# A scheduled GLA + RWKV-7 layer: PSUM-bank reads and DMA costs in the scheduler's account, new scheduling numbers, and the edge column copied before the shift

## The chip, the cores and the metric

The kernel runs on one core of one Trainium2 chip. The metric is device time in microseconds (us) of one execution, lower being better. TensorE is called PE here, VectorE is DVE, ScalarE is ACT, GpSimd is POOL, and SP is SyncE, whose instruction queue issues every DMA of this kernel. All data is fp32. Most projections run as three fp32r matmuls per block of weights, high and low parts of weights and inputs being kept apart.

## The reference

One layer of a hybrid decoder: 1024 prompt tokens and 8 sample tokens are projected by one large matrix, go through a gated linear attention branch (4 heads) and an RWKV-7 branch (16 heads), are merged under two sigmoid gates, projected once more and normalised.

```python
p = jnp.einsum('btd,dn->btn', x, w_in)
p_gla, p_rwkv, p_gate = _split(p, (GLA_COLS, RWKV_COLS, GATE_COLS))
...
o_gla, S_gla = _gla_chunked(...)          # chunked causal gated linear attention
...
prev = jnp.concatenate([shift0[:, None, :], p_rwkv[:, :-1]], axis=1)
pr = p_rwkv + (prev - p_rwkv) * rwkv_mu   # token shift: the part that one edit touches
...
y, S_rwkv = _rwkv7_scan(rh, hr(w), kh, vh, kk, hr(a), S_rwkv0)
...
m = (jax.nn.sigmoid(gate_a) * jnp.einsum('btc,cd->btd', o_gla, w_up_gla)
     + jax.nn.sigmoid(gate_b) * jnp.einsum('btc,cd->btd', o_rwkv, w_up_rwkv))
out = jnp.einsum('btd,de->bte', m, w_out)
y_out = _layernorm(DEEPNORM_ALPHA * x + out, ln_g, ln_b, LN_EPS)
```

## The kernel before

**Work and tiling.** Features lie on partitions and tokens on the free axis. The tokens go in two passes: pass 0 has 512 prompt tokens and the 8 sample tokens, cut in tiles of 256 and 264 columns (266 with the lead of the token shift), and pass 1 has the other 512 in one tile. In each pass a list of blocks (`make_plan`, line 1765) names the 128-row blocks of the big projection in order: per pair of RWKV heads (8 pairs) its r, k and v rows, per GLA head its q, k and v rows, the gate rows, and so on. `blocks` (line 726) walks the list: per tile it takes a PSUM bank (`proj`, of which there are 2, or `big`, of which there are 5), and runs 8 input blocks times 3 matmuls into it, the weights being read from four `wpart` buffers of half a block each. Then an evacuating stream reads the bank with ACT and DVE and frees it.

**Weights.** In pass 0 `load_w` (line 667) loads raw weights into `wraw`, ACT copies the high part into `wpart` (a CAST row of the profile), DVE subtracts for the low part, and the result is also stored to DRAM (`w<-wpart`). Pass 1 only reloads it (`wpart<-w`).

**The chain.** `chain` (line 1362) is the serial part of each pair of RWKV heads: 8 chunks, each with three dependent matmuls into the only `pch` bank. After the first, one copy `rh<-pch` by ACT or DVE; after the second, two copies `wide<-pch`, one for each half of the partitions, each by ACT or DVE; after the third, two adds on DVE. `front` (line 1183) prepares a pair: among much else it stores to DRAM (`LD<-gg`), loads back (`wide<-LD`), solves triangles on POOL (`Xt`, `X`) and sends results through DRAM (`XD`, `XT`, `Yd`).

**What sets the order.** No order is written out by hand. Every part of the work is a Python generator that yields one operation at a time, and `Order.run` (line 388) chooses, while the program is being built, which stream's operation is issued next on its engine. It keeps a clock per engine, prices each operation (`price`, line 156; `transfer`, line 217, for DMAs), and works out in `start` (line 351) when it could begin, from when its operands are written and from when its output buffer was last read. The key is that time less a priority (`PRIO`, and `FOR_PE` times a factor for matmuls). Where an operation has two engines to choose from (ACT or DVE, DVE or POOL), the one that would end first gets it, with a handicap (`BIAS` for DVE against ACT, `ASIDE` for POOL). The numbers at the head of the file feed this. Each engine then runs its list strictly in the order of issue, waiting at semaphores.

**The token shift.** `shift` (line 1121) evacuates a projected row of the RWKV branch: ACT writes (1 - mu) times the row, DVE adds mu times the row moved by one token, reading the same PSUM bank, and the last column of the bank is kept in `tail` by ACT, since pass 1 needs the column before its first token. There are 33 such rows in each pass.

**Other names.** `RAWS` (line 61) limits how many raw input blocks `load_x` holds; `EARLY_GATES` (line 70) is compared with an index that runs from 0 to 7 in `load_gates` (line 1577); `GATES` (line 71) says how many gate blocks stand behind each pair, for each pass.

Of the kernel before, what the change touches and what calls it, by code (L numbers as in the profile page):

```python
# [17 lines left out]
PSUM = bass.MemoryType.PSUM  # L18
DRAM = bass.MemoryType.DRAM
# [38 lines left out]
KEEP = 0  # L58
AHEAD = 6

RAWS = 6


WARM = 9
# [2 lines left out]
RANK = 16  # L67
LEAD = 2
SPARE_ROWS = 10
EARLY_GATES = 12  # L70
GATES = [[1, 1, 3, 0, 3, 2, 2, 4], [1, 1, 3, 2, 1, 3, 1, 4]]


HOP = {"P": 0.2, "D": 0.418, "G": 0.115, "V": 0.064, "A": 0.14}

SWITCH = 0.092
HOLD = 0.11
TABLE = 1.28

AGE = 2.117  # L80

SPARE = 0.411
LANDED = 0.648
BIAS = 0.133
ASIDE = 1.655

PRIO = {"evacuate": 0.333, "pair": 0.326, "turn": 0.426, "chain": 0.251, "norm": 0.026, "x": 0.745,
        "lora": 0.67, "rank": 1.291, "head": 0.198, "gate": -0.057, "w": 0.32, "out": 0.555, "state": 0.039,
        "block": 0.735}
FOR_PE = {"pair": 0.438, "turn": 2.001, "chain": 1.193, "norm": 0.187, "lora": 3.947, "rank": 2.131,  # L90
          "head": 0.435, "gate": 1.614, "state": 3.803, "out": 1.518}
STAND, SCARCE, PER_ROW = 0.037, 0.036, 0.042

URGENT = 2.628
SIGMOID, EXP = "sigmoid_and_others", "natural_log_exp_and_others"
SETS = {AF.Sigmoid: SIGMOID, AF.Tanh: SIGMOID, AF.Exp: EXP, AF.Ln: EXP}

# [58 lines left out]
def price(eng, name, out, args, ins):  # L156

    n = out.free_size()
    src = [x for x in ins if x.tensor.space != PSUM] if eng == "A" else ins
    if eng == "P":  # L160
        m = args[0].free_size()
        rows, cols = tiles(name, args)
        if name == "transpose":
            return 0.1095
        if args[0].dtype == F32R:
            return max(m / 1200, 0.0045 + n / 2256) if rows == cols == P else (m + n) / 1200
        if rows == cols == P:
            return 2 * max(m, n) / 1200 + 0.009
        if cols == 32 and n > 2 * P:
            return 0.017 + n / 2326  # L170
        return 0.1365 if cols == P else (0.0625 if cols == 64 else 0.142 if n > P else 0.088) if rows == P else 0.0285 if rows == cols == 64 else 0.5
    if eng == "S":
        return 0.56
    if eng == "A":
        extra = 0.5 * (len(ins) - 1) if src != ins else len(ins) - 1
        return 0.097 + n / 1200 + (0.042 if len(src) == len(ins) else 0.0) + 0.094 * extra
    wide = max([n, *(x.free_size() for x in ins)]) if name in ("tensor_reduce", "bn_stats", "bn_aggr") else n
    if eng == "V":
        if name == "tensor_tensor_scan":
            return 0.1 + n / 480  # L180
        if name == "transpose":
            return 0.17 + n / 960
        if name in ("tensor_copy", "copy", "memset") and ins and ins[0].tensor.space != PSUM:
            wide = wide / 2
        scalars = sum(x.free_size() == 1 for x in ins[1:]) if name in ("scalar_tensor_tensor", "tensor_scalar") else 0
        return 0.068 + wide / (480 if name == "copy_predicated" else 960) + 0.06 * scalars
    if name in ("tensor_scalar", "memset"):
        return 0.08 + n / 760
    return 0.1 + n / (300 if name == "tensor_copy" else 456)
# [27 lines left out]
def transfer(out, src):  # L217

    n = 4 * min(run_of(out), run_of(src), 512 if src.tensor.space == out.tensor.space else 1024)
    return out.nbytes() / n * (0.01 + n * 4.65e-5) / 16, 1.7 if out.tensor.space != DRAM else 1.2  # L220


class Engine:
# [43 lines left out]
class Order:  # L267
# [83 lines left out]
    def start(self, op):  # L351

        best = None
        for eng, fn, cost in op.ways:
            free, t = self.time[eng] + (SWITCH if eng == "P" and op.tiles != self.tiles else 0.0), 0.0
            for x in (*op.outs, *op.ins):
                at, by = self.ready.get(x.tensor.name, (0.0, None))
                if eng == "S" and by == "D" and x is op.out:
                    continue
                if by != eng:  # L360
                    at += HOP.get(by, 0.0) + (SPARE if eng == "P" and by in ("V", "A", "G") else LANDED if by == "D" else 0.0)
                elif eng != "P" and x is not op.out:
                    at += 0.13
                t = max(t, at)
            t = max(t, *(self.read.get(x.tensor.name, 0.0) for x in op.outs))
            if eng in op.port:
                free = max(free, self.port["G" if eng == "V" else "V"])
            late, t = free - t, max(t, free)
            if eng in "VA" and self.held(eng, op):
                cost += HOLD  # L370
            end = t + cost
            if len(op.ways) > 1:
                end += BIAS if eng == "V" and "A" in op.ways[0][0] else ASIDE if eng == "G" and "G" in op.port else 0.0
            if best is None or end < best[0]:
                best = end, t
                op.eng, op.fn, op.cost, op.late = eng, fn, cost, max(0.0, late)
        return best[1]
# [60 lines left out]
class Kern(Order):  # L438
# [682 lines left out]
    def shift(self, c, j, dst, smp=None):  # L1121

        i, A, V = c.i, self.A, self.V
# [3 lines left out]
        def ev(tt, t0, n, q):  # L1127
            np_ = n - c.ns if tt == last else n
            m = n if smp is not None else np_
            lead, e = (LEAD, 0) if tt else (0, 1)  # L1130
            yield lambda: "pv" in self.has
            if i:
                yield lambda: self.edged == NRC
                yield A.activation(dst[:, :1], q[:, :1], AF.Identity, scale=omu, bias=self.tail[:, 0, j:j + 1])
                yield A.activation(dst[:, 1:m], q[:, 1:m], AF.Copy, scale=omu)
            else:
                yield A.activation(dst[:, t0:t0 + m], q[:, lead:lead + m], AF.Copy, scale=omu)
            if i == 0 and tt == last:
                yield A.copy(self.tail[:, :, j], q[:, lead + np_ - 1:lead + n])
            yield V.scalar_tensor_tensor(dst[:, t0 + e:t0 + np_], q[:, lead + e - 1:lead + np_ - 1], mu,  # L1140
                                         dst[:, t0 + e:t0 + np_], ALU.mult, ALU.add)
            if i:
                yield A.copy(self.tail[:, 0, j:j + 1], q[:, n - 1:n])
            elif tt == last:
                self.edged += 1
                if self.edged == NRC:
                    o = PV["mu"][0]
                    yield V.tensor_mul(self.tail[:, 0], self.tail[:, 0], self.pv[:, o:o + NRC])
            if i == 0 and tt == last and smp is not None:
                yield V.scalar_tensor_tensor(smp, self.shT[:, j], mu, dst[:, HT:c.n], ALU.mult, ALU.add)  # L1150
# [754 lines left out]
```

## Time and profile before

| | |
|---|---|
| Median of 3 runs | 1454.28 us (1448.78 to 1454.93) |
| The profiled execution's own time | 1452.62 us |
| Its span, first to last instruction | 1450.8 us |
| DVE busy | 1065.5 us, 2184 instructions |
| ACT busy | 812.0 us, 2019 instructions |
| POOL busy | 385.3 us, 1146 instructions |
| DMA queue, share of 16 engines | 74.2% |

The profiled execution's time lies 1.8 us above its span. PE is almost always busy, so the numbers to read are PE's idle stretches: the view of waits lists them for one engine, by the instruction that ended each wait. A timeline row gives start and duration in us, the engine, the operation, what it writes and reads, and in brackets the idle time before it with what ended that.

### The profile page before, as it was taken

Reading aid. Unit: us, or ns where it says so; the run is one execution under the profiler, and the core shown is the slowest. Engines: PE = TensorE matmul, PEld = TensorE weight load, DVE = VectorE, ACT = ScalarE, POOL = GpSimd, SP = SyncE. Lnnn points to the kernel's source line nnn. Section 1 sums busy time; section 2 is a strip of 40 time slices with the busy share of each in tenths; the row PEclk is TensorE's granted clock in tenths of the full one; section 3 lists DMA queues with packets and bytes.
Section 4 is the critical chain, followed back from the end, with each engine's and each line's share of the span. In section 5 each row is a group of like instructions: output and inputs, shape, how many; then the busy total and the mean of one; then the engine's idle time right before and its main releaser. Section 6 shows DMA issues by size and latency. Waiting matters only on the chain.

```text
span 1450.8 us, 30348 instructions
## 1 busy us (share of the span) xinstructions
PE 1425.3 (98%) x10640; PEld 1251.5 (86%) x10640; DVE 1065.5 (73%) x2184; ACT 812.0 (56%) x2019; POOL 385.3 (27%) x1146
## 2 busy tenths in 40 slices
PE   9999999999999999999999999999999999999997
PEld 8999989999989999878887777887778898898786
DVE  7687578948894778577859786887788655666585
ACT  6565657665757486465564635464556655644210
POOL 1063315150615060505151314324141510000000
PEclk9999999999999999999999999999999999999999
DMA  9788779688877897768576578767786787798732
GB/s 334 254 278 274 234 268 300 225 252 299 284 227 244 279 325 253 205 207 230 176 193 210 147 202 215 235 167 204 212 244 201 227 250 248 238 303 275 260 111 87
DMA packets 284788, 340.12 MB, mean 234 GB/s; under 512 B 159027, under 2 KB 174524, under 8 KB 284636
## 3 DMA queue, kind: packets, MB, share of 16 engines
q1 hardware_dynamic: 284636, 338.18, 74.2%
q8 instruction: 85, 1.39, 0.4%
q14 instruction: 67, 0.55, 0.1%
HBM read 210.03 MB, written 127.00 MB: 232 GB/s over the span
## 4 chain that ended last, share of the span: by engine, by line
PE 83%; DVE 6%; DMA 5%; ACT 3%; SPq 1%; issue 1%; DVEq 0%; ACTq 0%
PE proj L234 52%; PE big L234 26%; PE pch L234 6%; DVE row L234 2%; SPq L234 1%; ACT row L234 1%; DMA wraw<-w_in 1%; DVE wide L234 1%; DMA wpart<-w 1%; DVE gg L234 1%; DMA w<-wpart 1%; DVE wpart L234 1%; DMA gla_s<-row 0%; DMA row<-vd 0%; DMA shift_s<-sto 0%
## 5 line engine op out<-in xcount | busy, mean ns | idle before, releaser
L234 PE MATMUL proj<-xh,wpart 128*128 128x512 f32 (+3 forms) x3680 | 902.2, 329 | 5.7 <-DMA wpart<-w 2.8
L234 PEld LDWEIGHTS proj<-xh,wpart 128*128 128x128 f32 x3680 | 612.8, 188 | 57.7 <-issue 7.6
L234 PE MATMUL proj<-xl,wpart 128*128 128x512 f32 (+3 forms) x1840 | 603.9, 328 | 0.0
L234 PEld LDWEIGHTS proj<-xl,wpart 128*128 128x128 f32 x1840 | 346.7, 188 | 26.0 <-issue 3.3
L234 POOL TENSOR_TENSOR Xt<-X,wide 128x60 f32<-128x60 f32 (+24 forms) x496 | 166.6, 336 | 376.4 <-DMA wide<-LD 191.8
L234 DVE TENSOR_TENSOR wpart<-wraw,wpart 128x512 fp32r<-128x512 f32 x210 | 145.5, 700 | 68.9 <-ACT wpart L234 65.7
L234 ACT CAST wpart<-wraw 128x512 fp32r<-128x512 f32 x210 | 129.2, 620 | 117.4 <-PE proj L234 43.4
L234 DVE TENSOR_TENSOR row<-row 128x512 f32<-128x512 f32 (+8 forms) x339 | 176.4, 532 | 10.8 <-ACT row L234 5.4
L234 POOL TENSOR_TENSOR X<-X,Xt 128x60 f32<-128x60 f32 (+24 forms) x496 | 171.3, 345 | 38.7
L234 ACT ACTIVATE row<-row 128x512 f32<-128x512 f32 (+3 forms) x229 | 137.6, 610 | 14.3 <-DVE row L234 6.8
L234 PE MATMUL big<-xh,wpart 128*128 128x256 f32 (+3 forms) x592 | 136.3, 318 | 0.0
L234 POOL TENSOR_TENSOR row<-row 128x512 f32<-128x512 f32 (+5 forms) x30 | 27.3, 919 | 347.9 <-DVE row L234 195.4
L234 PEld LDWEIGHTS big<-xh,wpart 128*128 128x128 f32 x592 | 98.1, 189 | 7.6 <-issue 0.8
L234 ACT COPY row<-big 128x128 f32<-128x128 f32 (+6 forms) x188 | 61.0, 346 | 61.8 <-PE big L234 52.0
L234 PE MATMUL big<-xl,wpart 128*128 128x256 f32 (+3 forms) x296 | 93.6, 316 | 0.6 <-DVE xl L234 0.6
L234 DVE TENSOR_TENSOR wide<-pch,gg 64x65 f32<-64x65 f32 x224 | 49.6, 222 | 58.3 <-PE pch L234 55.7
L234 ACT COPY rh<-pch 128x130 f32<-128x130 f32 x113 | 30.3, 268 | 107.6 <-PE pch L234 107.2
L234 DVE SCALAR_TENSOR_TENSOR row<-proj,pv,row 128x255 f32<-128x255 f32 (+1 forms) x95 | 54.4, 573 | 34.1 <-ACT row L234 25.4
L234 PE MATMUL big<-row 128*64 128x64 f32 (+5 forms) x680 | 69.7, 287 | 0.5 <-DVE row L234 0.4
L234 ACT COPY wide<-pch 64x65 f32<-64x65 f32 x213 | 44.2, 208 | 44.5 <-PE pch L234 40.5
L234 ACT ACTIVATE row<-proj,omu 128x256 f32<-128x256 f32 (+1 forms) x95 | 51.8, 545 | 25.1 <-PE proj L234 24.5
L416 ACT ACT_TABLE_LOAD x50 | 64.2, 1283 | 0.8
(216 smaller groups left out, 2044.9 us busy)
## 6 DMA issues: line engine op xcount, KB each, us to landing
w<-wpart SPq DMA_DIRECT2D x146, 512.0 KB
wpart<-w SPq DMA_DIRECT2D x146, 512.0 KB
wraw<-w_in SPq DMA_DIRECT2D x146, 256.0 KB
wide<-LD SPq DMA_DIRECT2D x64, 128.0 KB
BT<-row SPq DMA_DIRECT2D x32, 256.0 KB
wide<-BT SPq DMA_DIRECT2D x64, 128.0 KB
wraw<-w_up_gla SPq DMA_DIRECT2D x32, 256.0 KB
row<-w_out SPq DMA_DIRECT2D x32, 256.0 KB
```

Of the source, the lines that this page charges most:

```text
L234: ways.append((eng, lambda call=call: call(out, *args, **kw), price(eng, name, out, args, ins)))
L416: self.nc.scalar.preload_act_table_set(self.table)
```

## The change

The diff has three parts. The first is in the scheduler's account: `start` now also lets an operation that reads PSUM begin only after earlier readers of the same bank; `transfer` makes loads with a broadcast source 2.2 times as long and loads of at most 32 packets of over 2 KB 1.45 times, and stores to DRAM slightly shorter; the issue of a DMA is priced at 0.64 or 0.48 by its number of dimensions in place of 0.56; ACT's fixed cost is lowered from 0.097 to 0.065; a dependent operation on the same engine is spaced by a number for each engine. The second is a new set of scheduling numbers, among them `RAWS`, `GATES` and all priorities. The third is in `shift`: in pass 1 the last column is copied to `tail` ahead of DVE's read of the bank, no longer behind it.

```diff
-RAWS = 6
+RAWS = 5
...
-EARLY_GATES = 12
-GATES = [[1, 1, 3, 0, 3, 2, 2, 4], [1, 1, 3, 2, 1, 3, 1, 4]]
+EARLY_GATES = 16
+GATES = [[3, 1, 3, 1, 2, 3, 2, 1], [2, 1, 3, 5, 0, 1, 4, 0]]
...
+AFTER = {"A": 0.13, "V": 0.13, "G": 0.147, "S": 0.13}
...
-BIAS = 0.133
-ASIDE = 1.655
...
+BIAS = 0.148
+ASIDE = 1.497
...
     if eng == "S":
-        return 0.56
+        return 0.64 if max(sum(int(m) > 1 for _, m in x.ap) for x in (out, args[0])) > 2 else 0.48
     if eng == "A":
...
-        return 0.097 + n / 1200 + (0.042 if len(src) == len(ins) else 0.0) + 0.094 * extra
+        return 0.065 + n / 1200 + (0.042 if len(src) == len(ins) else 0.0) + 0.094 * extra
...
-    return out.nbytes() / n * (0.01 + n * 4.65e-5) / 16, 1.7 if out.tensor.space != DRAM else 1.2
+    packets = out.nbytes() / n
+    slow = 2.2 if any(int(s) == 0 and int(m) > 1 for s, m in src.ap) else 1.45 if packets <= 32 and n > 2048 else 1.0
+    if out.tensor.space == DRAM:
+        return packets * (0.01 + n * 4.2e-5) / 16, 1.2
+    return slow * packets * (0.01 + n * 4.65e-5) / 16, 1.7
...
                 elif eng != "P" and x is not op.out:
-                    at += 0.13
+                    at += AFTER[eng]
                 t = max(t, at)
-            t = max(t, *(self.read.get(x.tensor.name, 0.0) for x in op.outs))
+            t = max(t, *(self.read.get(x.tensor.name, 0.0) for x in (*op.outs, *(y for y in op.ins if y.space == PSUM))))
...
-            if i == 0 and tt == last:
+            if i:
+                yield A.copy(self.tail[:, 0, j:j + 1], q[:, n - 1:n])
+            elif tt == last:
                 yield A.copy(self.tail[:, :, j], q[:, lead + np_ - 1:lead + n])
             yield V.scalar_tensor_tensor(dst[:, t0 + e:t0 + np_], q[:, lead + e - 1:lead + np_ - 1], mu,
                                          dst[:, t0 + e:t0 + np_], ALU.mult, ALU.add)
-            if i:
-                yield A.copy(self.tail[:, 0, j:j + 1], q[:, n - 1:n])
-            elif tt == last:
+            if i == 0 and tt == last:
                 self.edged += 1
```

The program has the same 8925 matmuls before and after. DVE has 47 instructions fewer, ACT 45 more and 10 more table loads (61 in place of 51). Of the 128 copies `rh<-pch`, ACT had 113 and has 125; of the 256 copies `wide<-pch`, ACT had 213 and has 237. Chunks whose two `wide<-pch` copies are split between the engines go from 13 to 7. PE changes its tile size 230 times before and 223 times now.

**First place: ACT in pass 0, at the ninth `rh<-pch` of the chains.** What stands in brackets are the semaphores waited for, DMAHW being those of DMAs. Before:

```order
L234 CAST wpart<-wraw 128x512 [waits DMAHW6_49,DMAHW3_49]
L234 ACTIVATE row<-row 128x256 [waits DMAHW7_49]
L234 COPY rh<-pch 128x130 [waits PE_49]
L234 ACTIVATE gg<-wide,pc 128x130 [waits Activation_49,Pool_49]
L234 COPY row<-proj 128x256 [waits PE_49]
```

And now, from the cast ahead of the same copy on:

```order
L239 CAST wpart<-wraw 128x512 [waits DMAHW6_49,DMAHW7_49,PE_49,Activation_49]
L239 COPY wide<-vm 64x4
L239 ACTIVATE row<-proj 128x128 x2
L239 COPY wide<-vm 64x4
L239 ACTIVATE row<-proj 128x8
L239 COPY wide<-vm 64x4
L239 COPY rh<-pch 128x130 [waits PE_49]
```

The two rows that wait for DMAs stood directly ahead of the chain's copy; now a cast that does so stands six rows ahead of it.

**Second place: ACT in pass 1, at the eleventh edge column.** Before:

```order
L234 ACTIVATE row<-proj,tail,omu 128x1 [waits PE_49]
L234 ACTIVATE row<-proj,omu 128x511
L234 CAST part<-row 128x512 [waits DVE_49]
L234 COPY tail<-proj 128x1 [waits DVE_49]
L234 COPY rh<-pch 128x130 [waits PE_49]
```

And now:

```order
L239 ACTIVATE row<-proj,tail,omu 128x1 [waits PE_49]
L239 ACTIVATE row<-proj,omu 128x511
L239 COPY tail<-proj 128x1 [waits Activation_49]
L239 COPY rh<-pch 128x130 [waits PE_49]
```

The copy of the column waited for DVE's read of the bank with a chain copy behind it; now it follows ACT's own read of the bank.

**Third place: SP in pass 1, where the seventh pair's front stores and reloads `LD`.** Each row issues DMAs; `wpart<-w` are the weights of pass 1. Before:

```order
L234 DMA wpart<-w_1_7557 128x1024
L234 DMA S<-GS_161 128x256
L234 DMA LD_14632<-gg 32x8x32 x4
L234 DMA Ld<-gg 32x4x32 x4
L234 DMA wpart<-w_0_7611 128x1024
L234 DMA wide<-LD_14632 32x1024 x4
```

And now:

```order
L239 DMA wpart<-w_0_7477 128x1024
L239 DMA row<-OS 8x128 x6
L239 DMA wide<-Sp_167 64x65 x2
L239 DMA gla_p<-S 128x256
L239 DMA row<-OS 8x128 x2
L239 DMA row<-sg_105 128x520
L239 DMA wpart<-w_1_7533 128x1024
L239 DMA sg_132<-row 128x512
L239 DMA LD_14715<-gg 32x8x32 x4
L239 DMA Ld<-gg 32x4x32 x4
L239 DMA wide<-LD_14715 32x1024 x4
L239 DMA sg_133<-row 128x512
```

There were 9 other DMAs between two loads of weights and then the four `wide<-LD` behind the second load; now 12 stand ahead of one load, and behind it 15 (the last of them a `BT<-row`, not shown) ahead of the next. Over the whole of SP's list, stretches of 12 or more other DMAs between two loads `wpart<-w` were 6 and are 8.

More of the change, by code (lines that the diff above doesn't have):

```diff
@@ L78 @@
 TABLE = 1.28
-AGE = 2.117
+AGE = 1.487
 SPARE = 0.411
 LANDED = 0.648
-BIAS = 0.133
-ASIDE = 1.655
[L87 to L94, printed above, removed]
+BIAS = 0.148
+ASIDE = 1.497
+PRIO = {"evacuate": 0.383, "pair": 0.309, "turn": 0.598, "chain": 0.413, "norm": 0.266, "x": 0.754,
+        "lora": 0.377, "rank": 1.051, "head": 0.246, "gate": -0.174, "w": 0.3, "out": 0.424, "state": 0.186,
+        "block": 0.718}
+FOR_PE = {"pair": 1.47, "turn": 1.208, "chain": 0.733, "norm": 1.48, "lora": 1.838, "rank": 2.757,
+          "head": 0.983, "gate": 2.698, "state": 2.188, "out": 0}
+STAND, SCARCE, PER_ROW = 0.033, 0.043, 0.107
+URGENT = 1.952
 SIGMOID, EXP = "sigmoid_and_others", "natural_log_exp_and_others"
```

## The prediction

> **What bounds the kernel now.** I read the page first, for the span and the busy shares.
>
> ```profile
> span 1450.8 us, 30348 instructions
> PE 1425.3 (98%) x10640; PEld 1251.5 (86%) x10640; DVE 1065.5 (73%) x2184; ACT 812.0 (56%) x2019; POOL 385.3 (27%) x1146
> PE 83%; DVE 6%; DMA 5%; ACT 3%; SPq 1%; issue 1%; DVEq 0%; ACTq 0%
> ```
>
> PE is busy for 98% of the span, and the chain that ended last is 83% PE. No other engine is near its limit: ACT has 1450.8 - 812.0 = 639 us idle. PE's work doesn't change, so the time moves only by what PE waits. The view of PE's waits lists them; of its 14 rows these are the large ones.
>
> ```profile
> PE pch L234 <- DVE wide L234: 3.0, 5, 1.0
> PE pch L234 <- ACT rh L234: 3.0, 1, 3.0
> PE proj L234 <- DMA wpart<-w: 2.8, 2, 1.4
> PE proj L234 <- DVE row L234: 1.9, 2, 1.7
> PE pch L234 <- DVE rh L234: 1.2, 2, 0.6
> PE big L234 <- DVE Xd L234: 1.1, 1, 1.1
> PE pch L539 <- DVE warm L536: 1.1, 1, 1.1
> PE proj L234 <- ACT row L234: 0.6, 1, 0.6
> PE big L234 <- DVE xl L234: 0.6, 1, 0.6
> PE pch L234 <- ACT wide L234: 0.3, 1, 0.3
> PE big L234 <- ACT l2p L234: 0.2, 1, 0.2
> ```
>
> Each row gives the sum, the count and the longest. These add to 15.8 us, the three other rows to 1.3 more: about 17 us. The wait for `warm` is the start and stays, so some 16 us are all that any order can save by PE's idle time. The rest of PE's idle time is the end:
>
> ```profile
> 1443.04 0.28 PE L234 MATMUL big<-wpart,xl 128*128 128x256 f32 x1
> ```
>
> PE's last matmul ends at 1443.3, and 7.5 us of normalising and storing follow, which the last rows of ACT, DVE and PE in the new order repeat without change. So the question is which of about twenty small waits go, and how many new ones come. A change beyond 0.5% (about what a measurement of this kernel can tell from none) is 7.3 us, nearly half of all that waits.
>
> **Changes of PE's tile size.** They fall from 230 to 223.
>
> ```profile
> 642.09 0.40 PE L234 MATMUL proj<-xl,wpart 128*128 128x512 f32 x1
> 642.32 0.40 PE L234 MATMUL proj<-xh,wpart 128*128 128x512 f32 x1
> 642.65 2.06 PE L234 MATMUL big<-az,wide 64*128 64x128 f32 x32
> ```
>
> From start to start, equal matmuls take 0.23 us and the one ahead of a new tile size 0.33, so a change costs 0.10 us. Seven fewer give **-0.7 us**.
>
> **A cast that waits for a DMA ahead of the chain's copy.** The longest wait is at 188.87.
>
> ```profile
> 187.64 0.62 ACT L234 CAST wpart<-wraw 128x512 fp32r<-128x512 f32 x1 [4.45 <-DMA wraw<-w_in]
> 188.57 0.25 ACT L234 COPY rh<-pch 128x130 f32<-128x130 f32 x1
> 188.87 0.49 PE L234 MATMUL pch<-rh,XT 128*128 128x130 f32 x2 [3.00 <-ACT rh L234]
> ```
>
> ACT stands 4.45 us at the cast for weights that are late; the copy `rh` is queued behind it, and PE has no other work issued ahead of the chain's next matmul. In the first place of the order the cast now stands ahead of that copy with six small instructions between. By the copies here and below, 0.2 us each, that moves the cast about 1.2 us earlier, and as much of the same lateness is off the path. The gain lies between nothing (the weights are later still) and 3.0; I take **-1.2**, the part that the rows show.
>
> **Reads of one bank by two engines.** The scheduler now counts that DVE and ACT read a bank in turn. What that costs when it isn't counted:
>
> ```profile
> 219.55 0.48 DVE L234 SCALAR_TENSOR_TENSOR row<-proj,pv,row 128x256 f32<-128x256 f32 x1 [1.88 <-ACT tail L234]
> 221.15 0.46 PE L234 MATMUL pch<-wide,gg 128*128 128x130 f32 x2 [1.00 <-DVE wide L234]
> 415.30 0.36 PE L234 MATMUL proj<-xh,wpart 128*128 128x266 f32 x1 [1.67 <-DVE row L234]
> ```
>
> At 219.55 DVE stands 1.88 us until ACT has copied the edge column of that bank, the chain's adds come late behind it, and PE waits 1.00. At 415.30 PE waits 1.67 for a bank that DVE still reads. An account that knows of the turn puts other DVE work ahead; but at 219 ACT was itself late by a DMA, and at 415 DVE was behind, which no account of banks mends. Of 2.67 I take half, **-1.3** (ends 0 and -2.7).
>
> **The chain's copies go to ACT.**
>
> ```profile
> L234 ACT COPY rh<-pch x113: 242/268/301, 129.9 to 1241.9; 128x130 f32<-128x130 f32 x113
> L234 DVE COPY rh<-pch x15: 283/294/295, 203.0 to 1156.4; 128x130 f32<-128x130 f32 x15
> L234 ACT COPY wide<-pch x213: 193/208/221, 135.3 to 1243.6; 64x65 f32<-64x65 f32 x107
> L234 DVE COPY wide<-pch x43: 203/219/231, 131.1 to 1230.2; 64x65 f32<-64x65 f32 x43
> 509.74 0.49 PE L234 MATMUL pch<-rh,XT 128*128 128x130 f32 x2 [0.60 <-DVE rh L234]
> ```
>
> The two engines take the same time (268 against 294 ns, 208 against 219), so only the queue counts. Twelve `rh` and 24 `wide` copies leave DVE. The copy whose lateness cost 0.60 at 509.74 is now ACT's: **-0.6**; the other of the two, late in pass 1, stays on DVE. The load that ACT takes on, 36 copies of at most 0.27 us, lies in its 639 us of idle time.
>
> Here a rule of the Trainium skill speaks against the change. The rows first: a split pair.
>
> ```profile
> 879.34 0.21 ACT L234 COPY wide<-pch 64x65 f32<-64x65 f32 x1 [0.87 <-PE pch L234]
> 879.58 0.23 DVE L234 COPY wide<-pch 64x65 f32<-64x65 f32 x1 [2.60 <-ACT wide L234]
> ```
>
> ACT's copy ends at 879.55, DVE's starts at 879.58 and had waited for it; of the 13 split pairs none overlaps. So a split brings nothing, and that the splits fall to 7 costs nothing. The Trainium skill's page "PSUM — Partial Sum Buffer", section "PSUM bank collisions raise a hardware error", says that two engines may use one bank at once in different groups of 32 partitions, and these copies read different halves. By that rule six lost splits would cost six times about 0.2 us, and the sum would come out 1.2 us later; the trace disagrees for this program, and its rows decide.
>
> **Edge column first.** In pass 1 ACT no longer stands at the column for DVE's read.
>
> ```profile
> L234 ACT COPY tail<-proj x64: 150/160/189, 28.4 to 1119.3; 128x1 f32<-128x1 f32 x33, 128x9 f32<-128x9 f32 x31
>   DVE row L234: 25.8, 32
> 1317.02 5.57 PE proj L234 x24
> ```
>
> The second row is the idle time ahead of these copies, 25.8 us in 32 waits, all of it ACT's. DVE's read starts 0.16 us later, 33 times, and the bank comes free a copy earlier. But a tile of pass 1 keeps PE for 5.57 us (last row) with a second `proj` bank besides, and no wait of PE on a bank lies in pass 1. I take **0** (ends: -0.5, the rows `ACT wide` and `ACT l2p`, which are all that PE waits for ACT there, to 33 x 0.16 = +5.3, if DVE were always late; it is 73% busy). Moving ACT's column past DVE's queue adds no DMA.
>
> **Table loads.** Ten more.
>
> ```profile
> L416 ACT ACT_TABLE_LOAD x50 | 64.2, 1283 | 0.8
> ```
>
> That is 10 x 1.283 = 12.8 us on ACT, hidden by its idle time; nothing is listed as waiting for a load. Those with a chain copy within six rows behind them are 11 before and 11 now. I take **0**; the other end is +12.8, each load late for a chain copy.
>
> **DMAs and SP.**
>
> ```profile
> 992.12 2.62 SPq L234 DMA_DIRECT2D Ld<-gg  x4
> 994.86 1.92 SPq L234 DMA_DIRECT2D wide<-LD  x4
> 996.87 0.37 SPq L234 DMA_DIRECT2D wpart<-w  x1
> 1002.78 0.50 PE L234 MATMUL proj<-xh,wpart 128*128 128x512 f32 x1 [1.37 <-DMA wpart<-w]
> ```
>
> Four issues of `Ld` take 2.62 us (0.66 each), four of `wide<-LD` 1.92 (0.48), so the new prices 0.64 and 0.48 fit. Yet the weights' load at 996.87 had stood behind such a stretch, and PE waited 1.37 for them. Stretches of 12 or more are now 8, not 6; one of 6 ended so, and two more give 2 x 1.37 / 6 = **+0.5** (ends: none of them, and each of 8 at 3.0). The smaller `RAWS` and moved gate blocks cost 0: waits for new inputs are 0.6 in all (`xl`), and `GATES` moves 16 blocks per pass without adding one; without cover it would be those 0.6 at each of 7 changes of input, +3.6. `EARLY_GATES` does nothing, as its index ends at 7.
>
> **Sum.** -0.7 - 1.2 - 1.3 - 0.6 + 0.5 = -3.3. All other waits, 10 us, I keep: the same kinds of rows stand ahead of the chain's copies as before (a DMA wait within four rows: 260 of 608 before, 268 of 608 now), so those that vanish are dealt anew elsewhere. From the profiled execution's 1452.62 this gives **1449.3 us**; that execution lies 1.7 below the median, 1454.28, of runs from 1448.78 to 1454.93. Against the median it is -0.3%.
>
> **Rivals.** *The account works far better (faster).* All waits of the kinds now counted go: DMAs 2.8 + 3.0 + 1.1, banks 1.9 + 0.6 + 1.0, DVE's `rh` 1.2, together 11.6, and 0.7 of tile sizes: 1452.6 - 12.3 = 1440.3. For it: two thirds of PE's waits bear these names. Against: chain copies stand behind late casts as often as before. *SP holds back the weights (slower).* The third place puts 12 and then 15 issues around a single load. If each of 8 stretches ends in a wait of 2.8 to 3.0 us (the longest DMA-made wait here is 3.00), that is 22.4 to 24, less the 2.8 there were: about +20.4 on the forecast, 1469.7. It decides once a stretch outlasts the weights in hand, three half blocks of 2.8 us, 8.4 in all, by the DMA's landing; the stretch up to 996.87 did, by 1.37 us. Against: five of six did not. *The change does nothing that shows.* The tail copy frees only ACT, ties are dealt anew, and the time is 1452.6; for it speaks that PE already runs at 98%.
>
> **How the numbers follow.** Forecast 0.35; no effect 0.20, also within 0.5%; faster rival 0.32; slower rival 0.13. So faster by over 0.5% (below 1447.0) 0.32, within 0.55, slower (above 1461.6) 0.13. The range goes from the faster rival's 1440 to 1460: the forecast plus 12.8, less than the slower rival, for table loads. The forecast's own range is 1446 to 1454.
>
> **What would show it.** The wait of 3.0 for `rh` should shrink or vanish; ACT's 25.8 us at the column should be gone without any gain for PE; `proj <- DVE row` should fall below 1.9; `proj <- wpart<-w` should stay near 3. PE's waits should add to about 14 us in place of 17. The forecast is wrong if PE waits for `wpart<-w` more than four times, if chain copies wait behind table loads, or if PE's waits fall below 8.

## The result, and the profile after

The changed kernel takes **1438.84 us** (median of 4 runs, 1438.11 to 1439.84), the kernel before 1454.61 (4 runs, 1448.78 to 1455.73). The ratio is 0.990, with a 95% interval of 0.9873 to 0.9927: faster by about 15.8 us. The prediction was 1449.3, with less than 0.5% of change as the likeliest case, so the forecast was wrong by 10.5 us; the time lies 1.2 us below the low end of its range, and beside the faster rival's 1440.3. Profiled execution against profiled execution it is 1439.84 against 1452.62, 12.8 us less.

The page of the changed kernel, the rows that answer to those of before (lines of the code are 5 higher in its profile: L239 is what was L234):

```profile
span 1438.0 us, 30397 instructions
PE 1420.8 (99%) x10640; PEld 1250.2 (87%) x10640; DVE 1054.8 (73%) x2137; ACT 834.2 (58%) x2074; POOL 412.6 (29%) x1148
PE 81%; DVE 7%; ACT 4%; DMA 3%; issue 2%; POOL 2%; SPq 1%; DVEq 0%; ACTq 0%; POOLq 0%
```

PE is still what bounds it. The span is 12.8 us shorter, and two figures share that: PE's idle time was 1450.8 - 1425.3 = 25.5 us and is now 17.2, and PE's busy time, for the same 10640 matmuls, fell by 4.5. The view of PE's waits (sum, count, longest):

```profile
PE pch L239 <- DVE wide L239: 1.8, 4, 1.2
PE proj L239 <- DVE wpart L239: 1.4, 1, 1.4
PE proj L239 <- DVE row L239: 1.3, 1, 1.3
PE pch L544 <- DVE warm L541: 1.1, 1, 1.1
PE big L239 <- ACT part L239: 0.9, 1, 0.9
PE big L239 <- DVE xl L239: 0.5, 2, 0.2
PE big L239 <- DVE part L239: 0.4, 1, 0.4
PE big L239 <- DVE sto L239: 0.3, 1, 0.3
PE big L239 <- ACT xh L239: 0.3, 1, 0.3
PE big L239 <- ACT row L239: 0.3, 1, 0.3
PE big L239 <- DVE Xd L239: 0.3, 1, 0.3
PE big L239 <- DVE smp L239: 0.3, 1, 0.3
```

These add to 8.9 us, where those of before added to about 17. No row names a DMA any more (`wpart<-w` was 2.8), and none a copy `rh` (3.0 and 1.2 before). The end is as it was: PE's last matmul starts at 1430.16, and the span goes on for 7.5 us behind its end. The busy time's 4.5 us are for the most part waits too. In the rows at 642.09 and 642.32 that the prediction shows, matmuls that start 0.23 us apart are given 0.40 each, because their ends are modelled; so the first 0.17 us of a wait count as busy, and shorter waits aren't listed at all. Measured from start to start, the pairs of consecutive matmuls that are 0.2 us or more over the median of pairs of the same shapes, and for which the profile names a releaser, are 33 with 23.1 us before and 22 with 12.0 now: 11.1 of the 12.8. (The Trainium skill's page "Perfetto Trace Analysis", section "Identifying the Most-Contended Engine", says that the busy share of matmuls is no good measure of how close a kernel is to its limit, since they are pipelined; these numbers agree, as the busy time held some 3 us of waits, 11.1 less the 8.3 of idle time.)

What ACT waits for has changed with it. Its waits for the loads of weights, before and now:

```profile
ACT wpart L234 <- DMA wraw<-w_in: 20.0, 12, 4.4
ACT wpart L234 <- DMA wraw<-w_up_rwkv: 13.1, 7, 4.8
```

```profile
ACT wpart L239 <- DMA wraw<-w_up_gla: 8.0, 3, 3.9
ACT wpart L239 <- DMA wraw<-w_up_rwkv: 4.1, 2, 2.5
ACT wpart L239 <- DMA wraw<-w_in: 1.9, 3, 0.9
```

The weights of `w_in` come in time now: 1.9 us of ACT's waits in place of 20.0. And at the edge column it is DVE that waits until ACT has read the bank and copied the column (7.3 us in 9 waits before), not ACT for DVE's read:

```profile
L239 ACT COPY tail<-proj x64: 154/162/186, 27.7 to 1137.7; 128x1 f32<-128x1 f32 x33, 128x9 f32<-128x9 f32 x31
  DVE row L239: 26.1, 27
```

### The profile page after: what moved, and what is told of

It is laid out like the page before. It is cut to its first block, busy times and chain, and to the rows that moved or that the text cites. A ratio compares the mean times of both kernels' runs of the same rounds, so it can differ in the third digit from the quotient of the medians.

```text
span 1438.0 us, 30397 instructions
## 1 busy us (share of the span) xinstructions
PE 1420.8 (99%) x10640; PEld 1250.2 (87%) x10640; DVE 1054.8 (73%) x2137; ACT 834.2 (58%) x2074; POOL 412.6 (29%) x1148
## 4 chain that ended last, share of the span: by engine, by line
PE 81%; DVE 7%; ACT 4%; DMA 3%; issue 2%; POOL 2%; SPq 1%; DVEq 0%; ACTq 0%; POOLq 0%
PE proj L239 52%; PE big L239 24%; PE pch L239 5%; DVE row L239 3%; ACT row L239 3%; SPq L239 1%; DVE wide L239 1%; DVE gg L239 1%; POOL Xt L239 1%; POOL X L239 1%; DMA row<-o_rwkv 1%; DVE wpart L239 1%; ACT L421 1%; ACT wpart L239 1%; DMA XT<-XD 0%
## 5 line engine op out<-in xcount | busy, mean ns | idle before, releaser
L239 PE MATMUL proj<-xh,wpart 128*128 128x256 f32 (+3 forms) x3712 | 905.3, 328 | 2.9 <-DVE wpart L239 1.4
L239 PEld LDWEIGHTS proj<-xh,wpart 128*128 128x128 f32 x3712 | 618.5, 188 | 56.3 <-issue 7.3
L239 PE MATMUL proj<-xl,wpart 128*128 128x512 f32 (+3 forms) x1856 | 606.7, 327 | 0.0
L239 PEld LDWEIGHTS proj<-xl,wpart 128*128 128x128 f32 x1856 | 349.7, 188 | 25.1 <-issue 3.1
L239 POOL TENSOR_TENSOR Xt<-X,wide 128x60 f32<-128x60 f32 (+24 forms) x496 | 172.0, 347 | 399.5 <-DMA wide<-LD 292.9
L239 DVE TENSOR_TENSOR wpart<-wraw,wpart 128x512 fp32r<-128x512 f32 x210 | 145.5, 700 | 68.5 <-ACT wpart L239 63.7
L239 POOL TENSOR_TENSOR X<-X,Xt 128x60 f32<-128x60 f32 (+24 forms) x496 | 179.4, 362 | 38.5
L239 DVE TENSOR_TENSOR row<-row 128x512 f32<-128x512 f32 (+9 forms) x340 | 173.5, 525 | 13.6 <-ACT row L239 6.8
L239 ACT CAST wpart<-wraw 128x512 fp32r<-128x512 f32 x210 | 128.8, 619 | 84.4 <-PE proj L239 39.0
L239 ACT ACTIVATE row<-row 128x512 f32<-128x512 f32 (+5 forms) x229 | 137.9, 611 | 6.5 <-DVE row L239 2.7
L239 PE MATMUL big<-xh,wpart 128*128 128x256 f32 (+3 forms) x560 | 132.5, 324 | 0.3 <-ACT xh L239 0.3
L239 POOL TENSOR_TENSOR row<-row 128x512 f32<-128x512 f32 (+3 forms) x29 | 37.5, 1302 | 279.4 <-DVE row L239 162.1
L239 ACT COPY row<-big 64x256 f32<-64x256 f32 (+6 forms) x188 | 63.4, 350 | 73.0 <-PE big L239 67.1
L239 DVE TENSOR_TENSOR wide<-pch,gg 64x65 f32<-64x65 f32 x224 | 49.8, 222 | 75.4 <-PE pch L239 73.0
L239 PEld LDWEIGHTS big<-xh,wpart 128*128 128x128 f32 x560 | 93.5, 189 | 8.4 <-ACT xh L239 0.8
L239 ACT COPY rh<-pch 128x130 f32<-128x130 f32 x125 | 33.5, 268 | 103.9 <-PE pch L239 103.3
L239 PE MATMUL big<-xl,wpart 128*128 128x256 f32 (+3 forms) x280 | 90.2, 322 | 0.5 <-DVE xl L239 0.5
L239 DVE SCALAR_TENSOR_TENSOR row<-proj,pv,row 128x255 f32<-128x255 f32 (+1 forms) x95 | 54.5, 574 | 44.1 <-ACT tail L239 26.1
L239 ACT COPY wide<-pch 64x65 f32<-64x65 f32 x237 | 49.3, 208 | 48.9 <-PE pch L239 45.7
L239 PE MATMUL big<-row 128*64 128x64 f32 (+5 forms) x680 | 68.6, 287 | 0.3 <-ACT row L239 0.3
L239 ACT ACTIVATE row<-proj,omu 128x256 f32<-128x256 f32 (+1 forms) x95 | 51.7, 545 | 24.7 <-PE proj L239 23.9
```

Source lines behind the costliest of these rows:

```text
L239: ways.append((eng, lambda call=call: call(out, *args, **kw), price(eng, name, out, args, ins)))
```

## The experiments

Three theories. **1:** the scheduler's truer account gives an order with fewer waits. **2:** ACT's stand at the edge column (25.8 us before) made other things late, and the edit of `shift` is worth much. **3:** any edit deals the order anew, and the changed kernel is a good deal that its numbers were chosen for. "Dealt anew" means that the scheduler runs again on the changed inputs; "its own order" means that the order of issue is kept, but for the edit.

**The edge column alone, order kept.** In the order of before, the copy goes straight behind ACT's own read of the bank:

```diff
-                yield A.activation(dst[:, 1:m], q[:, 1:m], AF.Copy, scale=omu)
+                op = A.activation(dst[:, 1:m], q[:, 1:m], AF.Copy, scale=omu)
+                edge = A.copy(self.tail[:, 0, j:j + 1], q[:, n - 1:n])
+                op.ways = [(x, lambda f=f, g=edge.fn: (f(), g()), cost) for x, f, cost in op.ways]
+                edge.ways = [(x, lambda: None, cost) for x, _, cost in edge.ways]
+                yield op
...
-                yield A.copy(self.tail[:, 0, j:j + 1], q[:, n - 1:n])
+                yield edge
```

> The kernel before, with every engine's order kept, but in pass 1 the copy of the edge column is put straight behind ACT's own read of the bank. Theory 1 (the gain is made by the new order): PE doesn't wait there, so the time is that of before within 2 us, ACT's 25.8 us of idle time ahead of the column copies goes, and DVE gets a wait for ACT of about 0.16 us or more at some of the 33 rows. Theory 2 (ACT standing at the column made chain copies late): PE's waits for ACT (3.0 and 0.6 and 0.5 us, and 11.5 us on the weight loads) fall in pass 1 and the time falls by 3 us or more.

Measured: 1454.0 us, ratio 0.9981 (0.9964 to 0.9997). ACT's 25.8 us at the column are gone, for 2.7 us of gain, which the interval barely tells from none.

**And taken back in the new order.** The mirror image, in the order of the changed kernel: the copy is issued behind DVE's read.

```diff
+            op = V.scalar_tensor_tensor(dst[:, t0 + e:t0 + np_], q[:, lead + e - 1:lead + np_ - 1], mu,
+                                        dst[:, t0 + e:t0 + np_], ALU.mult, ALU.add)
             if i:
-                yield A.copy(self.tail[:, 0, j:j + 1], q[:, n - 1:n])
+                edge = A.copy(self.tail[:, 0, j:j + 1], q[:, n - 1:n])
+                op.ways = [(x, lambda f=f, g=edge.fn: (f(), g()), cost) for x, f, cost in op.ways]
+                edge.ways = [(x, lambda: None, cost) for x, _, cost in edge.ways]
+                yield edge
...
+            yield op
```

> The changed kernel, every engine's order kept, but in pass 1 the column is copied behind DVE's read again. Theory 1: within 2 us of the changed kernel (about 1439), ACT idles some 20 us more at the columns. Theory 2: most of the gain is lost, 1446 us or more.

Measured: 1447.5 us, ratio 0.9945 (0.993 to 0.996), 8.7 us over the changed kernel's median, by one instruction in 33 places. (The kernel before, run beside each group of experiments, had medians from 1453.42 to 1456.59, so differences across groups are uncertain by some 3 us.) The trace says how. First its waits of PE and its timeline (start, duration, engine, what is written and read, and in brackets the idle time before), then the same place of the changed kernel:

```profile
PE big L239 <- ACT l2p L239: 3.8, 4, 1.3
...
959.70 0.68 ACT L239 ACTIVATE row<-proj,omu 128x511 f32<-128x511 f32 x1
962.27 0.16 ACT L239 COPY tail<-proj 128x1 f32<-128x1 f32 x1 [1.90 <-DVE row L239]
962.33 0.41 ACT L239 CAST l2p<-l2s 128x256 fp32r<-128x256 f32 x1
...
962.79 0.50 PE L239 MATMUL big<-lw,l2p 128*128 128x512 f32 x1 [1.29 <-ACT l2p L239]
```

```profile
955.13 0.68 ACT L239 ACTIVATE row<-proj,omu 128x511 f32<-128x511 f32 x1
955.70 0.16 ACT L239 COPY tail<-proj 128x1 f32<-128x1 f32 x1
955.74 0.42 ACT L239 CAST l2p<-l2s 128x256 fp32r<-128x256 f32 x1
```

PE waits no longer for a bank than in the changed kernel (`proj <- DVE row` is 1.3 in both). It waits for the cast `l2p`, which stands in ACT's queue behind the copy: ACT stands 1.90 us until 962.27, and the cast comes 1.29 us too late for PE; in the changed kernel copy and cast follow ACT's read without a stand. Theory 2's mechanism is shown: `l2p` makes 3.8 of the 7.4 us between the two profiled executions, and the rest was not taken apart. The edit is worth 2.7 us in the order of before and 6.5 (by the ratios) to 8.7 (by the medians) in this one.

**Dealt anew by a trifle.** One number of the scheduler is moved by a thousandth, in each kernel.

```diff
-STAND, SCARCE, PER_ROW = 0.037, 0.036, 0.042
+STAND, SCARCE, PER_ROW = 0.038, 0.036, 0.042
```

> The kernel before with one number of the scheduler changed by a trifle (STAND 0.037 to 0.038), which deals the order anew without knowing anything better. If gains of this size come by chance (theory 3), the time moves by 5 us or more either way. If the new account and numbers are what gains (theory 1), it stays within 4 us of 1454.

```diff
-STAND, SCARCE, PER_ROW = 0.033, 0.043, 0.107
+STAND, SCARCE, PER_ROW = 0.034, 0.043, 0.107
```

> The changed kernel with the same trifle (STAND 0.033 to 0.034). Theory 1: it stays within 4 us of 1439. Theory 3 (a lucky order): it loses 5 us or more, towards 1447 to 1452.

Measured: the kernel before goes to 1476.35 (ratio 1.0141, 1.0111 to 1.0172), the changed one to 1444.06 (0.9923, 0.9902 to 0.9944). So a change that means nothing costs some 20 us in the one, which theory 1 had kept within 4, and 3 to 5 in the other, which decides nothing. In the first PE stands 7.71 us in one place. The profile names no releaser there (`issue`), but the matmul reads `Xd`, and the last of DVE's transposes into `Xd` ends 0.1 us ahead of it:

```profile
543.04 0.66 PE L234 MATMUL big<-Xd,Ld 128*32 128x128 f32 x8 [7.71 <-issue]
```

**One of the three parts undone, dealt anew.** The account of before under the new numbers; the numbers of before under the new account; the edge column copied last; and the edge column first in the kernel before.

```diff
-            t = max(t, *(self.read.get(x.tensor.name, 0.0) for x in (*op.outs, *(y for y in op.ins if y.space == PSUM))))
+            t = max(t, *(self.read.get(x.tensor.name, 0.0) for x in op.outs))
...
```

> The changed kernel with the scheduler's account of before (no turn of two engines on a bank, SP's issue at one price, old transfers and ACT price); the new numbers and the edge column first are kept, and the order is planned anew. Ratios are to the kernel before (changed kernel: 0.990). Theory 1 (the account makes the gain): back to before or worse, 0.998 or above, and PE waits again for wpart<-w and for a bank that DVE reads. Theory 2 (the edge column makes it): 0.990 to 0.993, as the column is still copied first. Theory 3 (any new deal of the order gives a draw of its own, and the changed kernel is a good draw that was picked): a draw, most likely 0.993 to 1.010, the waits of no kind in particular.

```diff
-RAWS = 5
+RAWS = 6
...
-PRIO = {"evacuate": 0.383, "pair": 0.309, "turn": 0.598, ...
+PRIO = {"evacuate": 0.333, "pair": 0.326, "turn": 0.426, ...
...
```

> The changed kernel with the table of numbers of before (RAWS, GATES, AGE, BIAS, ASIDE, PRIO, FOR_PE, STAND, SCARCE, PER_ROW, URGENT); the new account and the edge column first are kept. Theories 1 and 2: the gain stays, 0.990 to 0.994, since neither gives the numbers a part in it. Theory 3: a draw, most likely 0.993 to 1.010; the numbers were then picked for one deal, and without them the gain is mostly gone.

```diff
-            if i:
-                yield A.copy(self.tail[:, 0, j:j + 1], q[:, n - 1:n])
-            elif tt == last:
+            if i == 0 and tt == last:
                 yield A.copy(self.tail[:, :, j], q[:, lead + np_ - 1:lead + n])
...
+            if i:
+                yield A.copy(self.tail[:, 0, j:j + 1], q[:, n - 1:n])
...
```

> The changed kernel with the edge column of pass 1 copied behind DVE's read, as before, and the order planned with that. With the planned order of the changed kernel kept, the same edit cost 8 us (0.9945). Theory 2: 0.9945 or more, as ACT stands about 30 us at the column again and the planner can't put that elsewhere. Theory 1: 0.990 to 0.992, since an account that knows of the turn on a bank plans around it, and ACT's stand falls below 10 us. Theory 3: a draw, 0.990 to 1.005.

The last one is that diff in reverse, on the kernel before.

> The kernel before with the edge column of pass 1 copied first, and the order planned with that, all else as before. With the order of before kept, the same edit gave 0.9981. Theory 2: 0.992 to 0.998. Theory 1: 0.998 to 1.000. Theory 3: a draw around 1.000, 0.995 to 1.015, with ACT's stand at the column gone in any case.

Measured, with the ratio to before and its interval:

| | us | ratio |
|---|---|---|
| account undone | 1466.44 | 1.0098 (1.0065 to 1.0131) |
| numbers undone | 1478.52 | 1.0173 (1.0145 to 1.0202) |
| edge column last | 1445.19 | 0.9941 (0.9921 to 0.996) |
| before, edge column first | 1460.22 | 1.0054 (1.0033 to 1.0075) |

Without the account, or without the numbers, the result is slower than before, by 13 and by 25 us (before, beside them: 1453.42). The two belong together: the new numbers gain nothing under the old account, nor the new account with the old numbers. Theory 1 alone falls, and theory 2 alone too, since the column is still copied first in the two slow ones. Theory 3 fits best, though not in every case: numbers undone is worse than its range, which ended at 1.010. The edge column's part keeps its size under the new account and numbers, about 6 us dealt anew and 6.5 to 8.7 in a kept order; in the kernel before it gained 2.7 in a kept order and lost 6.8 to 7.9 dealt anew. Copied last and dealt anew, ACT still stands 18.4 us at it. With the numbers undone, about half of the loss is one stand between the passes:

```profile
556.17 0.80 PE L239 MATMUL big<-part,headsr 128*128 128x512 f32 x1 [11.31 <-ACT part L239]
```

Is a deal chance, then? The scheduler keeps a clock of its own while it issues, and the start that it gives PE's last matmul can be set beside the measured start, in us:

```text
                          scheduler   measured   difference
before                       1421.6     1443.0         21.4
before, trifle               1449.0     1461.7         12.7
before, column first         1429.6     1454.5         24.9
account undone               1438.1     1454.0         15.8
changed                      1419.5     1430.2         10.6
changed, trifle              1423.7     1434.0         10.3
column last                  1431.4     1435.5          4.2
numbers undone               1453.9     1468.7         14.8
```

The two columns roughly go together, and the two planned latest ended latest, so much of what a deal is worth was foreseen. But between before and changed only 2.1 us of the 12.9 were planned, and 10.8 are in the difference. With the old account (the first four) the chip is 18.7 us later than planned in the mean, with the new one 10.0. That the new account is nearer to the chip by some 9 us is what these eight orders show; with four each, whose differences run from 4.2 to 24.9, it is not more than likely.

**The longest wait of before.** In its own order, the chain's copy goes ahead of the cast whose weights are late, and the same with the edge column first. The edit holds back the cast, operation 2160 in the order of issue, and what needs it, until the copy, operation 2174, is issued.

```diff
+CAST, COPY = 2160, 2174
...
+        if self.n == CAST or self.late and self.n < COPY and self.names & {x.tensor.name for x in (*op.outs, *op.ins)}:
+            self.late.append(op.fn)
+            self.names |= {x.tensor.name for x in (*op.outs, *op.ins)}
+            return
+        op.fn()
+        if self.n == COPY:
+            for fn in self.late:
+                fn()
...
```

> The kernel before in its own order, but the chain's copy rh goes ahead of the cast that waits for late weights at 187.64 (and the activation between them too); the cast, and the subtraction on DVE that needs it, are issued right behind the copy. Nothing else moves. Theory A (a wait costs its length): the 3.0 us are gone, ratio 0.998, runs spread over 8 to 10 us as before. Theory B (a wait of 3 to 4 us also halves TensorE's clock for some 7 us, in the runs in which it is a little longer): 5 to 7 us less, 0.995 to 0.9965, mean clock 0.998 or more in every run in place of 0.995 to 0.998, spread under 4 us. Rival C (the lateness of the weights goes to the next matmuls that need them): 0.999 to 1.000, with a wait of 2 us or more for wpart some us later.

> The same, and the edge column of pass 1 copied first, in the order of before. If the two are additive: 0.9981 times the ratio of the run with the copy ahead of the late cast alone, so 0.993 to 0.9965. If the edge column's gain came through the same wait: no better than that run alone.

Measured: 1453.06 us, ratio 0.9999 (0.9983 to 1.0014), and 1450.37, ratio 0.9979 (0.9963 to 0.9995), the same as for the edge column alone. The runs of both still spread, over 7.0 and 9.8 us (9.4 before). The first one's timeline:

```profile
185.08 0.27 ACT L234 COPY rh<-pch 128x130 f32<-128x130 f32 x1 [1.03 <-PE pch L234]
189.17 0.62 ACT L234 CAST wpart<-wraw 128x512 fp32r<-128x512 f32 x1 [3.82 <-DMA wraw<-w_in]
190.84 0.42 ACT L234 COPY wide<-pch 64x65 f32<-64x65 f32 x2
...
191.31 0.49 PE L234 MATMUL pch<-wide 128*128 128x130 f32 x2 [3.38 <-ACT wide L234]
```

The copy runs at 185.08, in time, and PE's wait of 3.0 us is gone; but the cast still stands for its weights, the chain's next copy stands behind it, and PE waits 3.38 for that. Behind that wait the clock granted to PE (third column from the end) is low:

```profile
192.00:196.00 4.00, 4.00 (x23) 4.00 (x22) 3.97 (x7) 2.14 (x4) 0.00 (x0) 0.57 0.97 389
```

The lateness moves on by one link. The time is rival C's; the wait is not the one that it named, for `wpart` some us later, but the chain's own next copy. So what has to go is the lateness of the weights. Where that came from the windows of before show (length, busy time of PE, PEld, DVE, ACT and POOL, PE's clock, share of the DMA engines, GB/s):

```profile
184.50:186.50 2.00, 1.37 (x12) 1.16 (x10) 0.22 (x1) 0.00 (x0) 0.00 (x0) 1.00 0.63 125
186.50:188.50 2.00, 0.00 (x0) 0.00 (x0) 0.21 (x1) 0.86 (x2) 0.00 (x0) 1.00 1.02 407
```

For 2 us the DMA engines moved 125 GB/s at 63% busy, then 407 at 102%: 2.0 times the engine time for a byte. The slow stretch moves 0.25 MB, the size of one load `row<-vd`, which copies one row of DRAM to all 128 partitions (line 1044) and was issued at 182.25, just ahead of the weights at 182.81. By the trace's semaphores its sixteen parts land from 184.66 to 186.89 and those of the weights from 186.62 to 187.62. A factor of 2.2 for such loads is one of the things that the new account has. That this load makes the weights late is read from these rows; no run moved it, so it isn't shown. Nor is that the account brings them in time: ACT's waits for `w_in`, 20.0 us before, are 5.5 with the account undone and 3.8 in the kernel before with its trifle.

**What a wait of PE costs.** Into the changed kernel, in its own order, waits are put by doing the chain's copy `rh` over and over: 21 times at each of two places, or 34 times at one (`self.n` counts operations in the order of issue; the second kernel has `{6735: 34}`).

```diff
+REPEAT = {6735: 21, 9251: 21}
...
+        for _ in range(REPEAT.get(self.n, 1)):
+            op.fn()
```

> The changed kernel in its own order, with the chain's copy rh done 21 times over on ACT at two places, 557.74 and 837.49, where no wait is near; the output is the same. 20 more copies of about 0.19 us make the copy 3.8 us late, PE has 1.35 us of other work, so each place gives PE one wait of about 2.4 us. Theories A and B alike: 4.8 us more than the changed kernel (1443 to 1445), clock 1.00 in both places.

> The changed kernel in its own order, with the chain's copy rh done 34 times over at 557.74 alone: 33 x 0.19 = 6.3 us late, so one wait of about 4.9 us, as much as the two of the other run together. Theory A: 4.9 us more than the changed kernel, equal to the run with two waits. Theory B: 2.5 to 3.5 us beyond that (1446 to 1448), with the clock at 0.50 for 7 us from the wait's last part on.

Measured: 1452.78 us (1450.12 to 1454.35) and 1449.62 us (1448.16 to 1451.65), 13.9 and 10.8 over the changed kernel. A repeated copy takes 0.30 us, not 0.19, so the waits came out longer than meant, 4.55 and 4.58 in the one, 8.45 in the other; and the two waits, though hardly longer in sum, cost 3 us more than the one:

```profile
564.20 0.80 PE L239 MATMUL pch<-rh,XT 128*128 128x130 f32 x2 [4.55 <-ACT rh L239]
851.28 0.80 PE L239 MATMUL pch<-rh,XT 128*128 128x130 f32 x2 [4.58 <-ACT rh L239]
```

```profile
566.48 0.80 PE L239 MATMUL pch<-rh,XT 128*128 128x130 f32 x2 [8.45 <-ACT rh L239]
```

PE's other listed waits add to 8.3 us in the one and 8.8 in the other, against 8.9 in the changed kernel, so they don't make the difference. The windows of the first, then of the second:

```profile
560.00:562.00 2.00, 0.00 (x0) 0.00 (x0) 0.00 (x0) 1.81 (x7) 0.00 (x0) 1.00 0.00 0
562.00:564.00 2.00, 0.00 (x0) 0.00 (x0) 0.00 (x0) 1.78 (x8) 0.00 (x0) 0.61 0.00 0
564.00:569.00 5.00, 4.80 (x14) 3.56 (x16) 2.99 (x6) 2.25 (x7) 0.00 (x0) 0.50 0.40 104
569.00:571.00 2.00, 2.00 (x33) 1.88 (x33) 1.44 (x3) 0.55 (x2) 0.00 (x0) 0.93 0.35 135
```

```profile
560.00:566.00 6.00, 0.00 (x0) 0.00 (x0) 0.00 (x0) 5.36 (x21) 0.00 (x0) 0.57 0.00 0
566.00:571.00 5.00, 4.52 (x12) 3.37 (x12) 2.71 (x6) 2.50 (x8) 0.00 (x0) 0.50 0.36 97
571.00:573.00 2.00, 2.00 (x33) 1.86 (x32) 1.73 (x3) 0.55 (x2) 0.00 (x0) 0.98 0.40 154
```

During the wait the clock granted to PE falls to 0.50, and it stays there for 4.6 to 5.1 us of PE's work behind it. That costs half of those, about 2.4 us, once for each of these waits: 4.55 + 4.58 + 2 x 2.4 = 13.9 and 8.45 + 2.4 = 10.9, as measured. Theory A (a wait costs its length) falls, and of theory B the mechanism holds; its times don't, as it priced shorter waits. Shorter waits at the same places weren't measured, since the two of the first run were meant to be 2.4 us and weren't.

## Why the prediction was wrong

The prediction had the direction and a quarter of the size: 3.3 us where the profiled executions differ by 12.8. Of the 9.5 between, 5.6 lie in PE's listed waits, which fell by 8.2 in place of 2.6, and 3.8 in its busy time. That its range nearly reaches the time is owed to the rival whose 1440 it took for its low end, not to its own sum. (Its top end, "the forecast plus 12.8", would be 1462.1, not 1460.) None of its three signs of being wrong came: PE's waits stayed above 8, and it was wrong all the same.

**Changes of PE's tile size (-0.7).** Not measured apart; the busy time has room for it.

**The late cast (-1.2).** The right wait, the wrong mechanism. Moving the copy ahead of the cast is worth nothing (0.9999): the wait goes on to the chain's next copy. All of the 3.0 us went, and with them nearly all of ACT's waits for `w_in` (20.0 to 1.9): the weights come in time. Before, it often cost more than its 3.0 us: in the runs of before the mean granted clock is 0.994 to 0.998, in those of the changed kernel 0.998 or 0.999, and in the profiled execution of the order of before with the edge column first the wait was 4.12 us and the clock fell with it (5 us of it in the next row). The execution that the prediction was read from had kept 0.999. How much of the time this made isn't shown: clock and time of the runs of before go together only loosely (at 0.997 they take 1449.43 to 1455.67 us).

```profile
188.00:193.00 5.00, 4.54 (x20) 4.54 (x21) 4.97 (x9) 3.11 (x9) 0.00 (x0) 0.50 0.99 389
```

**Reads of one bank by two engines (-1.3).** `proj <- DVE row` fell from 1.9 to 1.3 and `pch <- DVE wide` from 3.0 to 1.8, together 1.8: near, as a size (0.5 more than foretold). Which line of the account did it wasn't tried by itself.

**The chain's copies (-0.6).** Right in kind, half the size: DVE made PE wait for `rh` twice; the prediction kept one of the two, and both are gone (1.2). Table loads cost 0, as taken: no chain copy is late behind one.

**DMAs and SP (+0.5).** Wrong in sign: `proj <- wpart<-w`, which should have stayed near 3, is gone: 2.8 less where 0.5 more was foretold. Of the listed waits it is the term furthest off. Which edit did it isn't shown; the wait is also 0.3 in the kernel before with its trifle and 1.0 with the account undone. With it the slower rival falls: the stretches of issues made no wait of PE.

**The edge column (0; ends -0.5 to +5.3).** A step that failed. The prediction looked for the column's cost at the bank, found PE never waiting for one in pass 1, and concluded that ACT's stand is ACT's own affair. What is queued behind ACT's copy it priced by the order of before alone, where PE hardly waited for it (`ACT l2p` 0.2, `ACT wide` 0.3), and there the edit is worth 2.7 us; in the new order the casts stand right behind it, and it is worth 6 to 8.7. A price from the trace of before holds for the order of before.

**All other waits (10 us, kept).** The step that failed by most. The sum kept what its terms left over of the rows that they name, on the ground that "those that vanish are dealt anew elsewhere". The rows that a term names (`ACT rh`, `DVE rh`, `proj <- DVE row`, `DVE wide`, `wpart<-w`) were 11.9 us before; they should have kept 9.3 and kept 3.1. They were not dealt anew: all other rows, `warm` among them, were 5.2 and are 5.8. "The same kinds of rows stand ahead of the chain's copies as before" counts neighbours, not lateness, and says nothing of how good the deal as a whole is. And the 4.5 us in PE's busy time were not in the "some 16 us" that it allowed any order to save, for those were read from listed idle time alone.

**The faster rival** came within 1.5 us (1440.3), with most of its claims: DMA-made waits gone, those at banks smaller, those for `rh` gone. Its reason, that the account works by itself, does not hold: with the numbers of before the same account gives 1478.52. Why this one pair of account and numbers gives so good an order stays open.

## What to carry to other kernels

Where a table of numbers steers a scheduler, the table, the scheduler's account and the code that it orders are one thing: undo each alone before crediting any, and read the scheduler's own end time, which foretold here the two worst orders, though not the gain. A wait on an engine is priced by what stands behind it in that engine's queue in the new order, not by who waits for its result in the old one. And moving work out from behind a late transfer only handed the wait to the next link here; the transfer had to come earlier.

## What the runs showed of the hardware

A wait of PE of 3.0 us left the clock alone (the profiled execution of before); one of 3.38 didn't (0.57 in the row from 192.00 on, of the kernel with the copy ahead of the cast), nor did one of 3.21 (of the kernel before with its trifle) or any of 4.1 and more. The Trainium skill's page "TensorE: Matmul & The Clock Gate", section "HAM oscillation — how this bites in real kernels", gives the rule of no idle gap of PE over some 3.4 us; these rows come near it. But a single gap isn't needed: with the account undone no wait there is over 2.21 us, PE was busy for 2.01 of 6 us, and the clock fell all the same:

```profile
548.00:554.00 6.00, 2.01 (x8) 1.18 (x7) 5.94 (x14) 3.40 (x10) 0.00 (x0) 0.78 0.47 162
554.00:557.00 3.00, 2.71 (x11) 2.41 (x11) 2.73 (x7) 1.05 (x3) 0.00 (x0) 0.50 0.58 233
```

The clock records of the 14 traces say more. Ahead of PE's last matmul each stretch at 0.50 lasts 3.41, 6.83, 10.24 or 13.65 us, whole multiples of 3.41, and in one execution the stretches begin a whole multiple apart (562.46 and 849.18 in the run with two waits: 84 x 3.413). Cut into such intervals, each of the 16 falls follows one in which PE was busy for at most 1.90 us; with 1.55 or less the clock always fell, between the two only sometimes. Before's wait of 3.0 us lay across two intervals, with 2.23 and 1.59 us of work, and was spared: what counts here is PE's work in an interval, and so also where a wait happens to lie. The price is half of PE's work in the stretch at 0.50, whatever the wait's length: about 2.4 us for those of 4.55, 4.58 and 8.45, 1.7 for that of 3.38, 3.1 for that of 3.21, and 2.2 for that of 11.31 with the numbers undone.

And the one load looked at that copies one row of DRAM to all partitions took the DMA engines 2.0 times as long for a byte as the traffic behind it (63% busy at 125 GB/s, then 102% at 407).
